# Second halves of the moving rows begin 1152 bytes on, with the padding behind each half

## The chip, the cores and the metric

One NeuronCore of one Trainium2 chip runs the whole program. The metric is the device time of one execution in microseconds (us); less is better. TensorE (PE in the rows) multiplies, VectorE (DVE) and ScalarE (ACT) do the elementwise work, GpSimd (POOL) does a little of it, and SyncE's queue (SP) issues the DMA transfers.

## The reference, cut to what matters

The reference is one inference step of a two-layer decoder trunk in float32, for 512 prompt tokens and 8 sample tokens that share all weights. Per layer:

```python
h = rmsnorm(x, W['norm_mix_w'][l])
(q, k, v, g, u, vm, om, ig, fg, z, xbc, dt, gate_r, gate_m, gate_s) = split_cols(h @ W['w_in'][l])
...
merged = (sigmoid(gate_r) * (y_r @ W['w_br_ret'][l])
          + sigmoid(gate_m) * (y_m @ W['w_br_ml'][l])
          + sigmoid(gate_s) * (y_s @ W['w_br_ssm'][l]))
x = x + merged @ W['w_out_mix'][l]
h = rmsnorm(x, W['norm_mem_w'][l])
x = x + mem_attention(h, mem_k, mem_v, W['mem_wq'][l], W['mem_wo'][l])
h = rmsnorm(x, W['norm_mlp_w'][l])
x = x + square(relu(h @ W['mlp_w1'][l])) @ W['mlp_w2'][l]
```

`y_r`, `y_m` and `y_s` come from three recurrent branches (retention, mLSTM, SSD). Nearly all arithmetic lies in the products of a 520-token activation with 1024-wide weight matrices.

## The kernel before, in words

Activations lie transposed: features on the 128 partitions, tokens along the free axis. The T = 520 columns are the L = 512 prompt tokens followed by the NB = 8 sample tokens. Products are made more exact than one float32r pass by splitting each operand into a high part and the remainder: `x = hi + lo`, `w = whi + wlo`, and the kernel sums `whi*xhi + whi*xlo + wlo*xhi`. The two parts of an activation stand in one tile, a "pair": `pair(tag)` (line 229) takes `[128, 2, 2, 576]` float32r, that is part (hi, lo), one of two row blocks, and a row of 576 columns of which the first 520 are used. Four tiles of the tag "h" and four of the tag "y" hold all such operands: the normed input, the branches' outputs, the merged gates, the attention's output, the hidden layer of the MLP. In the built program each of these tiles begins at a multiple of 256 bytes within a partition, and a row takes 2304 bytes.

`mmacc` (line 291) is the loop that nearly all PE work goes through. Per row block k it does three products (hi with hi, hi weights with lo input, lo weights with hi input), and each of them as two matmuls of HF = 260 columns, since a PSUM bank holds 512 float32:

```python
for j in range(2) if half is None else (half,):
    mm(ps[:, j, :HF] if half is None else ps[:, :HF], lhsT=w, rhs=x[:, j * HF:(j + 1) * HF],
```

So the matmuls alternate between a first half, read from the row's start, and a second half, read from byte 1040 of the row. Their results go to two PSUM banks. Every matmul loads its weights anew, also where the second half uses the same ones. `proj` (line 305) does 8 row blocks, 48 matmuls, into one such pair of banks. The MLP's second product (line 1788 on) does 4 row blocks, 24 matmuls. By these loops 19,872 matmuls of 260 columns read a pair's halves in alternation.

Three kinds of matmul read their moving operand otherwise. The mLSTM's q and k products from the tile `ucp` (in `proj_M`, lines 1016 to 1031) do six matmuls on one half and then six on the other, into one bank each; their rows are 520 columns with nothing between them. The memory keys (`mem_kv`, line 432 on) take 256 columns from row blocks of 256 columns, into one bank. The last group of the last layer's MLP (`last_group`, line 1727) takes columns 256 to 520 and then 0 to 256 of the pair's rows, into one bank.

The pairs are written by `split` (line 314: an ACT copy to hi, a DVE subtraction to lo), by `to_pair` (line 691), by `prep` and the merging of the gates (lines 1422 to 1435), and in the attention by lines 1515 and 1516. In most of them one ACT and one DVE instruction cover all 520 columns. In the retention and mLSTM branches and in the attention they cover the 512 prompt columns, and separate small DVE instructions write the 8 sample columns later.

PE's instructions stand in the order in which the program was written: a clock inside the recording (`clk`, advanced by each `mm`) decides when the generators of the branches put their instructions between the projections. The other engines' order is set by a scheduler from due times.

Of the kernel before, what the change touches and what calls it, by code (L numbers as in the profile page):

```python
# [17 lines left out]
NB = 8  # L18
T = L + NB
HF = T // 2  # L20
NT = 8
PITCH = 576
DEPTH = 2
C = 128
NC = L // C
# [87 lines left out]
def tile_trunk(ctx: ExitStack, tc: tile.TileContext, I, O):  # L113
# [69 lines left out]
    def tl(pool, shape, tag, bufs=None, dt=F32):  # L183
        return pool.tile(shape, dt, tag=tag, name=nm(tag), bufs=bufs)
# [42 lines left out]
    pmask = spar[:, 128:136]  # L227

    def pair(tag):
        return tl(act, [128, 2, 2, PITCH], tag, 4, F32R)[:, :, :, 0:T]  # L230

    def pieces(pairs):
        r = []
        for t in pairs:
            for k in range(2):
                r.append((t[:, 0, k, :], t[:, 1, k, :]))
        return r


    class Weights:  # L240
# [50 lines left out]
    def mmacc(ps, wl, xl, k0=0, k1=None, half=None, cols_=None):  # L291
        n = len(wl)
        for k in range(k0, n if k1 is None else k1):
            wh, wlo = wl[k]
            xh, xlo = xl[k]
            for m, (w, x) in enumerate(((wh, xh), (wh, xlo), (wlo, xh))):
                if cols_ is not None:
                    mm(ps, lhsT=w, rhs=x[:, cols_], start=(k == 0 and m == 0), stop=(k == n - 1 and m == 2))
                    continue
                for j in range(2) if half is None else (half,):  # L300
                    mm(ps[:, j, :HF] if half is None else ps[:, :HF], lhsT=w, rhs=x[:, j * HF:(j + 1) * HF],
                       start=(k == 0 and m == 0), stop=(k == n - 1 and m == 2))
            tick()

# [28 lines left out]
    def col(name, i):  # L333
        o = COLO[name] + i
        return cols[:, o:o + 1]
# [137 lines left out]
    def layer(l, mp, load_x):  # L473
# [17 lines left out]
        def g_norm():  # L491
            xt, ssq = yield from load_x()
            yield 4.0 if l else 2.2
            d = diag_cols(rms_cols([ssq.acc], 0, EPS))
            yield 5.29 if l else 4.3
            rb = rstd_row(d)
            for k in range(NT):
                hf = tl(un, [128, T], "yb", 2)
                V.scalar_tensor_tensor(out=hf, in0=xt[k], scalar=col("mix", k), in1=rb, op0=ALU.mult, op1=ALU.mult)
                split(hf, hx[k][0], hx[k][1])  # L500
                if l > 0:
                    st_.dma_start(out=xscr[:, k, :], in_=xt[k])

# [184 lines left out]
        def sel_b(b):  # L688
            return sel[:, b:b + 1].to_broadcast([128, 128])

        def to_pair(pt, k, f32t, s=None):
            s = slice(0, L) if s is None else s
            split(f32t, pt[:, 0, k, s], pt[:, 1, k, s])


        cs = tl(un, [128, 2080], "ucp", 1)
# [114 lines left out]
        def normalise(h, ysb, mv, rs, gt, kind, yps):  # L811
            nb = tl(sm, [128, NC], "nb", 2)
            V.scalar_tensor_tensor(out=nb, in0=mv[:, :, 0], scalar=-1.0, in1=rs, op0=ALU.mult, op1=ALU.mult)
            for c in range(NC):
                A.activation(out=ysb[:, c, 0:256], in_=ysb[:, c, 0:256], func=AF.Identity, scale=rs[:, c:c + 1], bias=nb[:, c:c + 1])
            yield 13.87
            stash = kind == "M" and not flags["br0"]
            if stash:
                while held[0] == 2:
                    yield 0.5  # L820
                held[0] += 1
                keep = tl(un, [128, 2, T], "gs", 2)
            else:
                yp = pair("y")
                yps[h] = yp
            for i in range(2):
                ps = pa([128, NC, 128])
                for c in range(NC):
                    tr(out=ps[:, c, :], in_=ysb[:, c, i * 128:(i + 1) * 128], identity=ident)
                yb = keep[:, i, :] if stash else tl(un, [128, T], "yb", 2)  # L830
                psf = ps.rearrange("p a b -> p (a b)")
                if kind == "R":
                    V.scalar_tensor_tensor(out=yb[:, 0:L], in0=psf, scalar=nwr[:, 2 * h + i:2 * h + i + 1], in1=gt[:, i, 0:L],
                                           op0=ALU.mult, op1=ALU.mult)
                else:
                    A.activation(out=yb[:, 0:L], in_=psf, func=AF.Copy, scale=nwr[:, 8 + 2 * h + i:9 + 2 * h + i])
                    V.scalar_tensor_tensor(out=yb[:, 0:L], in0=gt[:, i, 0:L], scalar=1.0, in1=yb[:, 0:L], op0=ALU.add, op1=ALU.mult)
                if not stash:
                    to_pair(yp, i, yb[:, 0:L])
            if stash:  # L840
                yield from unstash(keep, "br0", h, yps, slice(0, L))

        def unstash(keep, flag, h, yps, sl):
            while not flags[flag]:
                yield 0.5
            yps[h] = pair("y")
            for i in range(2):
                to_pair(yps[h], i, keep[:, i, sl], sl)
            held[0] -= 1

        def g_smp_R(h, vs, qkw):
# [52 lines left out]
        def smp_finish(ys, gs, nwo, yps):  # L904
            for i in range(2):
                V.tensor_tensor(out=ys[:, i, :, :], in0=ys[:, i, :, :],
                                in1=nwr[:, nwo:nwo + 8].rearrange("p (h i) -> p h i", i=2)[:, :, i:i + 1].to_broadcast([128, 4, NB]), op=ALU.mult)
            V.tensor_tensor(out=ys, in0=ys, in1=gs, op=ALU.mult)
            for h in range(4):
                V.tensor_copy(out=yps[h][:, 0, :, L:T], in_=ys[:, :, h, :])  # L910
                V.tensor_tensor(out=yps[h][:, 1, :, L:T], in0=ys[:, :, h, :], in1=yps[h][:, 0, :, L:T].bitcast(F32), op=ALU.subtract)

        def g_end_R(ints, smps, yps):
            while not all(s.done for s in smps):
# [78 lines left out]
        def proj_M(h):  # L993
# [22 lines left out]
            hi, lo = W.get(l, ("wqk", h))  # L1016
            q = tl(un, [128, 2, EXT], "pA", 1)
            k = tl(un, [128, 2, T], "pD", 1)
            xl = [(ucp[:, 0, i, :], ucp[:, 1, i, :]) for i in range(2)]
            for w in range(2):  # L1020
                for i in range(2):
                    sl = [slice(512 * w + 256 * kk + 128 * i, 512 * w + 256 * kk + 128 * i + 128) for kk in range(2)]
# [187 lines left out]
        def g_int_S(g, X, BC, sz, xs, s_smp, yps):  # L1210
# [115 lines left out]
            for i in range(2):  # L1326
                j = 2 * g + i
                yb = keep[:, i, :] if stash else tl(un, [128, T], "yb", 2)
                V.scalar_tensor_tensor(out=yb[:, 0:L], in0=yz[:, i, 0:L], scalar=col("ssmn", j), in1=p1, op0=ALU.mult, op1=ALU.mult)
                V.scalar_tensor_tensor(out=yb[:, L:T], in0=yz[:, i, L:T], scalar=col("ssmn", j), in1=p2, op0=ALU.mult, op1=ALU.mult)  # L1330
                if not stash:
                    to_pair(yp, i, yb, slice(0, T))
            if stash:
                yield from unstash(keep, "br1", g, yps, slice(0, T))

        def g_smp_S(g, xs, bcs):
            smp_scr(2, g, bcs, 2, 0.5)
# [72 lines left out]
        for j in range(8):  # L1410
            ph[0] = "br2."
            m0_ = tl(un, [128, T], "row", 2)
            ld.dma_start(out=m0_, in_=mscr[:, j, :])
            if j < 2:
                ps, wl = part[j]
                mmacc(ps, wl, yx, 6, 8)
                ps = ps[:, :, :HF]
            else:
                ps = proj(l, ("br", 2, j), yx)
            th = ths[j]  # L1420
            with soon():
                V.scalar_tensor_tensor(out=h2(th), in0=h2(th), scalar=1.0, in1=ps, op0=ALU.add, op1=ALU.mult)
            V.tensor_tensor(out=th, in0=th, in1=m0_, op=ALU.add)
            A.activation(out=mx[j][0], in_=th, func=AF.Copy, scale=0.5)
            V.scalar_tensor_tensor(out=mx[j][1], in0=th, scalar=0.5, in1=mx[j][0].bitcast(F32), op0=ALU.mult, op1=ALU.subtract)


        xs_ = XTiles()
# [2 lines left out]
        ax = pieces(ap_)  # L1431

        def prep(j, x, wname, dst, acc):
            A.activation(out=dst[j][0], in_=x, func=AF.Copy, scale=col(wname, j))
            V.scalar_tensor_tensor(out=dst[j][1], in0=x, scalar=col(wname, j), in1=dst[j][0].bitcast(F32), op0=ALU.mult, op1=ALU.subtract)
            acc.add(x)


# [25 lines left out]
        def g_att_p():  # L1464
# [44 lines left out]
            def outp(h, i):  # L1509
# [2 lines left out]
                for mt in range(2):  # L1512
                    mm(ps, lhsT=Vt[:, mt, i * 128:(i + 1) * 128], rhs=pT[h][:, mt, 0:512], start=(mt == 0), stop=(mt == 1))
                with soon():
                    A.activation(out=op[:, 0, i, 0:L], in_=ps, func=AF.Copy)
                    V.tensor_tensor(out=op[:, 1, i, 0:L], in0=ps, in1=op[:, 0, i, 0:L].bitcast(F32), op=ALU.subtract)  # L1516

            while 1 not in qs_ or not s_rq.done:
                yield 0.5
# [28 lines left out]
        def g_att_s(par):  # L1548
# [21 lines left out]
            for hi_, h in enumerate(heads):  # L1570
# [43 lines left out]
                        acc = tl(sm, [128, 2, NB], "o8", 2)  # L1614
                        yield 2.84
                with soon():
                    V.tensor_copy(out=op[:, 0, :, L:T], in_=acc)
                    V.tensor_tensor(out=op[:, 1, :, L:T], in0=acc, in1=op[:, 0, :, L:T].bitcast(F32), op=ALU.subtract)
                done_s.add(h)

        KT = []
# [142 lines left out]
        for g in range(9):  # L1764
            if g < 8:
                hps = [pair("h") for _ in range(2)]
                hid[g] = pieces(hps)
                pend = []
                for i in range(4):
                    ps = proj(l, ("w1", 4 * g + i), fx)  # L1770
# [5 lines left out]
                    for ps in pend:  # L1776
# [2 lines left out]
                        with soon():  # L1779
                            V.scalar_tensor_tensor(out=h2(rt), in0=ps, scalar=0.0, in1=h2(rbox[0]), op0=ALU.max, op1=ALU.mult)  # L1780
                        A.activation(out=rt, in_=rt, func=AF.Square)
                        split(rt, hid[g][ii][0], hid[g][ii][1])
                    pend = []
            if g > 0:
                hxg = hid.pop(g - 1)
# [214 lines left out]
```

## Time and profile before

| | |
|---|---|
| median of 3 runs | 2958.45 us (2951.89 to 2959.17) |
| the profiled execution | 2957.6 us |
| its span, first to last instruction | 2955.9 us |
| PE busy | 2900.0 us, 98% of the span |
| PE weight loads busy | 2826.5 us, 96% |
| DVE busy | 1865.5 us, 63% |
| ACT busy | 1309.0 us, 44% |
| granted TensorE clock, mean | 0.995 of full speed |

Busy times of PE are those of matmuls whose recorded durations overlap (a matmul of 260 columns is recorded as some 280 ns and the next one starts some 118 ns later), so PE's pace is read from the starts, not from the durations.

### The profile page before, as it was taken

To read this page: it belongs to the slowest core of one execution; us is meant where nothing else is said; L and a number is where in the kernel's file an instruction comes from. 1 tells how busy PE (TensorE), PEld (TensorE's weight loads), DVE (VectorE), ACT (ScalarE), POOL (GpSimd) and SP (SyncE) were. 2 spreads that over 40 slices of the span, in tenths; PEclk is the share of its full clock that TensorE was granted. 3 is DMA by queue.
4 is the path that set the end of the run, shared out by engine and by line. 5 is a ranking of instruction groups with operands and counts; after the bars stand their busy time and mean duration, and the time that the engine had idled before them with its cause. 6 is when DMAs were issued, how large, how long until landed. Compare 5 with 4: busy or idle time off the path is not lost. (4 is left out here: it accounts for less than half of the span.)

```text
span 2955.9 us, 57336 instructions
## 1 busy us (share of the span) xinstructions
PE 2900.0 (98%) x23334; PEld 2826.5 (96%) x23334; DVE 1865.5 (63%) x4254; ACT 1309.0 (44%) x2367; POOL 127.6 (4%) x388
## 2 busy tenths in 40 slices
PE   8999999999999999999999999999999999999998
PEld 7999999999999879999999999999999997899998
DVE  6677646776755665444576775568777556644445
ACT  5445445555533653322353454355545246432322
POOL 0001001100000000000000000010000000000000
PEclk9999999999999999999999999999999999999999
DMA  5445635454554642222454465445545445422221
GB/s 195 153 166 171 209 120 182 167 172 148 178 174 148 199 146 94 93 97 97 140 170 161 131 209 187 167 140 188 167 147 185 132 150 189 135 94 95 99 94 65
DMA packets 153112, 439.97 MB, mean 149 GB/s; under 512 B 18376, under 2 KB 31816, under 8 KB 152816
## 3 DMA queue, kind: packets, MB, share of 16 engines
q1 hardware_dynamic: 152848, 436.31, 44.8%
q8 instruction: 183, 3.00, 0.4%
q14 instruction: 81, 0.66, 0.1%
HBM read 380.43 MB, written 57.90 MB: 148 GB/s over the span
## 5 line engine op out<-in xcount | busy, mean ns | idle before, releaser
L272 ACT ACTIVATE mlp.wh<-mlp.raw 128x1024 fp32r<-128x1024 f32 x125 | 132.4, 1059 | 467.5 <-PE mlp.pp L170 451.6
L170 PE MATMUL mlp.pp<-mlp.h,mlp.wh 128*128 128x260 f32 (+2 forms) x1984 | 313.7, 280 | 0.0
L170 PE MATMUL mlp.pp<-kv.y,mlp.wh 128*128 128x260 f32 x1984 | 312.9, 280 | 0.0
L170 PEld LDWEIGHTS mlp.pp<-mlp.h,mlp.wh 128*128 128x128 f32 x1984 | 268.0, 188 | 0.0
L170 PEld LDWEIGHTS mlp.pp<-kv.y,mlp.wh 128*128 128x128 f32 x1984 | 266.9, 188 | 1.0 <-issue 1.0
L170 PE MATMUL mlp.pp<-mlp.h,mlp.wl 128*128 128x260 f32 (+2 forms) x992 | 199.0, 280 | 0.0
L170 PE MATMUL mlp.pp<-kv.y,mlp.wl 128*128 128x260 f32 x992 | 196.4, 280 | 0.0
L273 DVE TENSOR_TENSOR mlp.wl<-mlp.raw,mlp.wh 128x1024 fp32r<-128x1024 f32 x125 | 153.1, 1225 | 19.8 <-ACT mlp.wh L272 19.8
L1780 DVE SCALAR_TENSOR_TENSOR mlp.cc<-mlp.pp,rb.Cst 128x520 f32<-128x520 f32 x64 | 44.7, 699 | 180.1 <-PE mlp.pp L170 175.8
L170 PEld LDWEIGHTS mlp.pp<-mlp.h,mlp.wl 128*128 128x128 f32 x992 | 152.1, 188 | 0.0
L170 PEld LDWEIGHTS mlp.pp<-kv.y,mlp.wl 128*128 128x128 f32 x992 | 150.9, 188 | 0.0
L170 PE MATMUL Rp.pp<-mlp.h,Rp.wh 128*128 128x260 f32 x736 | 120.9, 286 | 2.2 <-DVE Rp.ext L719 2.0
L170 PE MATMUL Rp.pp<-h,Rp.wh 128*128 128x260 f32 x736 | 120.7, 286 | 1.5 <-DVE Rp.ext L719 0.8
L273 DVE TENSOR_TENSOR Mp.wl<-Mp.raw,Mp.wh 128x1024 fp32r<-128x1024 f32 x56 | 68.5, 1223 | 75.7 <-ACT Mp.wh L272 75.5
L170 PE MATMUL Sp.pp<-mlp.h,Sp.wh 128*128 128x260 f32 x640 | 105.0, 286 | 0.0
L170 PE MATMUL Sp.pp<-h,Sp.wh 128*128 128x260 f32 x640 | 104.9, 286 | 0.0
L272 ACT ACTIVATE br.wh<-br.raw 128x1024 fp32r<-128x1024 f32 x64 | 67.6, 1056 | 84.1 <-PE br.pp L170 81.9
L170 PEld LDWEIGHTS Rp.pp<-mlp.h,Rp.wh 128*128 128x128 f32 x736 | 101.4, 188 | 3.2 <-issue 2.2
L170 PE MATMUL Mp.pp<-mlp.h,Mp.wh 128*128 128x260 f32 x640 | 103.7, 284 | 0.0
L170 PEld LDWEIGHTS Rp.pp<-h,Rp.wh 128*128 128x128 f32 x736 | 101.0, 188 | 2.7 <-issue 1.0
L170 PE MATMUL Mp.pp<-h,Mp.wh 128*128 128x260 f32 x640 | 103.6, 284 | 0.0
L273 DVE TENSOR_TENSOR br.wl<-br.raw,br.wh 128x1024 fp32r<-128x1024 f32 x64 | 78.2, 1222 | 24.1 <-ACT br.wh L272 23.9
(826 smaller groups left out, 7882.3 us busy)
## 6 DMA issues: line engine op xcount, KB each, us to landing
mlp.raw<-wall SPq DMA_DIRECT2D x125, 512.0 KB, 3.5
br.raw<-wall SPq DMA_DIRECT2D x64, 512.0 KB, 3.6
Mp.raw<-wall SPq DMA_DIRECT2D x56, 512.0 KB, 3.5
Rp.raw<-wall SPq DMA_DIRECT2D x48, 512.0 KB, 3.6
Sp.raw<-wall SPq DMA_DIRECT2D x48, 512.0 KB, 3.6
Ms.st<-s_ml SPq DMA_DIRECT2D x32, 512.0 KB, 4.8
Ms.bc<-sscr SPq DMA_DIRECT2D x64, 256.0 KB, 4.7
o_mlC_s<-Ms.st SPq DMA_DIRECT2D x32, 512.0 KB, 4.9
```

The costliest lines, as they stand in the source:

```text
L170: PE.matmul(out, lhsT=lhsT, rhs=rhs, start=start, stop=stop)
L272: A.activation(out=hi[:, s], in_=t[:, s], func=AF.Copy)
L273: V.tensor_tensor(out=lo[:, s], in0=t[:, s], in1=hi[:, s].bitcast(F32), op=ALU.subtract)
L1780: V.scalar_tensor_tensor(out=h2(rt), in0=ps, scalar=0.0, in1=h2(rbox[0]), op0=ALU.max, op1=ALU.mult)
```

## The change

The row of 576 columns becomes two halves of HP = 288 columns, each with 260 used and 28 of padding. The second half now begins 1152 bytes after the first, in place of 1040. The tile's size, its place and the row pitch of 2304 bytes stay. All that reads or writes a pair follows:

- `mmacc` takes the half by an index of its own (`x[:, j, :]`), and `pieces` hands out views of shape `[128, 2, 260]`.
- Writers of all 520 columns write two runs of 260 in one instruction.
- Writers of the 512 prompt columns (retention, mLSTM, attention) write 260 and then 252 columns, in two instructions on ACT and two on DVE.
- The last group of the last layer's MLP keeps rows of 520 columns without a gap (`halved=False`).
- The tile `ucp` keeps its layout; it is only viewed as two halves.

```diff
@@ -18,8 +18,8 @@
 HF = T // 2
+HP = 288
 NT = 8
-PITCH = 576
@@ -227,14 +227,20 @@
     def pair(tag):
-        return tl(act, [128, 2, 2, PITCH], tag, 4, F32R)[:, :, :, 0:T]
-
-    def pieces(pairs):
+
+        return tl(act, [128, 2, 2, 2 * HP], tag, 4, F32R)
+
+    def halves(row):
+        return row.rearrange("p (j n) -> p j n", j=2)[:, :, 0:HF]
+
+    def pieces(pairs, halved=True):
         r = []
         for t in pairs:
             for k in range(2):
-                r.append((t[:, 0, k, :], t[:, 1, k, :]))
+                r.append(tuple(halves(t[:, s, k, :]) if halved else t[:, s, k, 0:T] for s in range(2)))
         return r
+
+    SMP = slice(L + HP - HF, T + HP - HF)
@@ -298,7 +304,7 @@
-                    mm(ps[:, j, :HF] if half is None else ps[:, :HF], lhsT=w, rhs=x[:, j * HF:(j + 1) * HF],
+                    mm(ps[:, j, :HF] if half is None else ps[:, :HF], lhsT=w, rhs=x[:, j, :],
@@ -688,9 +694,13 @@
-        def to_pair(pt, k, f32t, s=None):
-            s = slice(0, L) if s is None else s
-            split(f32t, pt[:, 0, k, s], pt[:, 1, k, s])
+        def to_pair(pt, k, f32t, samples=False):
+
+            if samples:
+                split(h2(f32t), halves(pt[:, 0, k, :]), halves(pt[:, 1, k, :]))
+                return
+            for a, b, o in ((0, HF, 0), (HF, L, HP - HF)):
+                split(f32t[:, a:b], pt[:, 0, k, a + o:b + o], pt[:, 1, k, a + o:b + o])
@@ -1512,8 +1522,7 @@
                 with soon():
-                    A.activation(out=op[:, 0, i, 0:L], in_=ps, func=AF.Copy)
-                    V.tensor_tensor(out=op[:, 1, i, 0:L], in0=ps, in1=op[:, 0, i, 0:L].bitcast(F32), op=ALU.subtract)
+                    to_pair(op, i, ps)
@@ -1764,7 +1773,7 @@
-                hid[g] = pieces(hps)
+                hid[g] = pieces(hps, halved=not (g == 7 and l == DEPTH - 1))
```

The other hunks replace `split(hf, ...)` by `split(h2(hf), ...)` and the slice `L:T` by `SMP` in the same way. PE's instructions are the same in number, shape and order; only their addresses differ. POOL's are the same as well. ACT and DVE get 48 instructions more each, from 48 splits of prompt columns.

One of the places where an instruction becomes two is the attention's output of the first head, on ACT. `Qp.h` is the pair, `Ap.pa` the PSUM tile that the attention's product was written to. Before:

```order
674 L1612 ACTIVATE br2.bcE_11247<-As.row_12396,As.mxs_12395 8x256
675 L1515 ACTIVATE Qp.h_11934<-Ap.pa_12403 128x512
676 L1493 ACTIVATE Ap.E_12415,Ap.sm_1846_12414<-Ap.pa_12408,Ap.mx_1845_12413,br2.rq_1647_11238 128x256 x2
677 L1599 ACTIVATE As.gs_11279,As.o_1842_12402<-As.gs_11279 128x256
678 L1496 ACTIVATE Ap.E_12415<-Ap.E_12415,Ap.sm_1846_12414 128x256 x2
679 L1515 ACTIVATE Qp.h_11934<-Ap.pa_12439 128x512
```

And after the change:

```order
693 L1621 ACTIVATE br2.bcE_11279<-As.row_12428,As.mxs_12427 8x256
694 L321 ACTIVATE Qp.h_11966<-Ap.pa_12435 128x260
695 L321 ACTIVATE Qp.h_11966<-Ap.pa_12435 128x252
696 L1503 ACTIVATE Ap.E_12449,Ap.sm_1846_12448<-Ap.pa_12442,Ap.mx_1845_12447,br2.rq_1647_11270 128x256 x2
697 L1608 ACTIVATE As.gs_11311,As.o_1842_12434<-As.gs_11311 128x256
698 L1506 ACTIVATE Ap.E_12449<-Ap.E_12449,Ap.sm_1846_12448 128x256 x2
699 L321 ACTIVATE Qp.h_11966<-Ap.pa_12473 128x260
700 L1608 ACTIVATE As.gs_11311,As.o_1842_12434<-As.gs_11311 128x256 x2
701 L321 ACTIVATE Qp.h_11966<-Ap.pa_12473 128x252
```

Each copy of 512 columns became two, and two of the sample stream's instructions now stand between the pieces of the second one.

## Rows read from the trace of the kernel before

**Rows 1.** The page's head: busy time, and the granted clock in 40 slices.

```profile
span 2955.9 us, 57336 instructions
...
PE 2900.0 (98%) x23334; PEld 2826.5 (96%) x23334; DVE 1865.5 (63%) x4254; ACT 1309.0 (44%) x2367; POOL 127.6 (4%) x388
...
PEclk9999999999999999999999999999999999999999
```

**Rows 2.** Timeline of PE in layer 1's MLP: start us, us, instructions merged, count.

```profile
2700.06 0.40 PE L170 MATMUL mlp.pp<-kv.y,mlp.wl 128*128 128x260 f32 x2
2700.29 0.63 PE L170 MATMUL mlp.pp<-kv.y,mlp.wh 128*128 128x260 f32 x4
2700.76 0.40 PE L170 MATMUL mlp.pp<-kv.y,mlp.wl 128*128 128x260 f32 x2
2700.99 0.63 PE L170 MATMUL mlp.pp<-kv.y,mlp.wh 128*128 128x260 f32 x4
2701.46 0.40 PE L170 MATMUL mlp.pp<-kv.y,mlp.wl 128*128 128x260 f32 x2
```

**Rows 3.** The same view in the third branch's output product of layer 1.

```profile
2349.73 0.40 PE L170 MATMUL br2.pp<-Si.y,br2.wl 128*128 128x260 f32 x2
2349.97 0.64 PE L170 MATMUL br2.pp<-Si.y,br2.wh 128*128 128x260 f32 x4
2350.45 0.40 PE L170 MATMUL br2.pp<-Si.y,br2.wl 128*128 128x260 f32 x2
...
2351.89 0.40 PE L170 MATMUL br2.pp<-Si.y,br2.wl 128*128 128x260 f32 x2
```

**Rows 4.** Busy time by stretches: from:to, us, PE, PEld, DVE, ACT, POOL busy (instructions), clock.

```profile
1140.00:1480.00 340.00, 340.00 (x2916) 340.00 (x2915) 166.76 (x194) 105.97 (x132) 0.00 (x0) 1.00 0.32 105
2340.00:2400.00 60.00, 60.00 (x502) 60.00 (x501) 33.03 (x42) 20.70 (x27) 0.00 (x0) 1.00 0.48 139
```

**Rows 5.** Timeline of PE: 256 columns, all read from multiples of 1024 bytes.

```profile
1484.14 0.28 PE L170 MATMUL kv.pp<-mlp.y,kv.wl 128*128 128x256 f32 x1
...
1485.22 0.28 PE L170 MATMUL kv.pp<-mlp.y,kv.wl 128*128 128x256 f32 x1
```

**Rows 6.** Timeline of PE in the last group: 264 columns from byte 1024 of a row.

```profile
2921.19 0.29 PE L170 MATMUL mlp.pp<-mlp.h,mlp.pC 128*128 128x264 f32 x1
...
2926.29 0.28 PE L170 MATMUL mlp.pp<-mlp.h,mlp.pC 128*128 128x264 f32 x1
```

**Rows 7.** Timeline of PE: q and k products from `ucp`, one half at a time.

```profile
265.06 0.28 PE L170 MATMUL Mp.pa<-Mp.ucp,Mp.wl 128*128 128x260 f32 x1
...
266.50 0.28 PE L170 MATMUL Mp.pa<-Mp.ucp,Mp.wl 128*128 128x260 f32 x1
```

**Rows 8.** Timeline of PE at the end: matmuls of one column, each with a weight load.

```profile
2929.79 0.58 PE L170 MATMUL fin.pa<-onesc,mlp.yb 128*128 128x1 f32 x4
2930.24 0.36 PE L170 MATMUL fin.pa<-onesc,mlp.cst 128*128 128x1 f32 x2
2930.46 0.58 PE L170 MATMUL fin.pa<-onesc,mlp.yb 128*128 128x1 f32 x4
```

**Rows 9.** Splits on ACT and DVE (lines 315, 316): duration ns min/median/max, first and last start.

```profile
L315 ACT ACTIVATE Ri.y<-Ri.yb x16: 612/632/635, 144.9 to 1726.3; 128x512 fp32r<-128x512 f32 x16
L315 ACT ACTIVATE mv.cc<-mv.row x4: 400/408/420, 947.6 to 2406.0; 128x256 fp32r<-128x256 f32 x4
L316 DVE TENSOR_TENSOR mlp.h<-mlp.cc,mlp.h x64: 690/700/702, 1132.1 to 2895.1; 128x520 fp32r<-128x520 f32 x64
L316 DVE TENSOR_TENSOR Ri.y<-Ri.yb,Ri.y x16: 672/683/684, 145.9 to 1727.0; 128x512 fp32r<-128x512 f32 x16
L316 DVE TENSOR_TENSOR mv.cc<-mv.row,mv.cc x4: 417/424/426, 948.0 to 2406.5; 128x256 fp32r<-128x256 f32 x4
```

**Rows 10.** Groups by line: an instruction of two runs of 260, read from two banks.

```profile
L1780 DVE SCALAR_TENSOR_TENSOR mlp.cc<-mlp.pp,rb.Cst 128x520 f32<-128x520 f32 x64 | 44.7, 699 | 180.1 <-PE mlp.pp L170 175.8
```

**Rows 11.** Who waited for the tile `Qp.h`, us and times.

```profile
  PEld wo.pp L170: 2.0, 5
  PE wo.pp L170: 0.4, 2
```

More of the change, by code (lines that the diff above doesn't have):

```diff
@@ L499, in g_norm @@
                 V.scalar_tensor_tensor(out=hf, in0=xt[k], scalar=col("mix", k), in1=rb, op0=ALU.mult, op1=ALU.mult)
-                split(hf, hx[k][0], hx[k][1])
+                split(h2(hf), hx[k][0], hx[k][1])
                 if l > 0:
@@ L840, in normalise, with unstash @@
             if stash:
-                yield from unstash(keep, "br0", h, yps, slice(0, L))
-        def unstash(keep, flag, h, yps, sl):
+                yield from unstash(keep, "br0", h, yps, False)
+        def unstash(keep, flag, h, yps, samples):
             while not flags[flag]:
@@ L847, in unstash @@
             for i in range(2):
-                to_pair(yps[h], i, keep[:, i, sl], sl)
+                to_pair(yps[h], i, keep[:, i, 0:T if samples else L], samples)
             held[0] -= 1
@@ L909, in smp_finish @@
             for h in range(4):
-                V.tensor_copy(out=yps[h][:, 0, :, L:T], in_=ys[:, :, h, :])
-                V.tensor_tensor(out=yps[h][:, 1, :, L:T], in0=ys[:, :, h, :], in1=yps[h][:, 0, :, L:T].bitcast(F32), op=ALU.subtract)
+                V.tensor_copy(out=yps[h][:, 0, :, SMP], in_=ys[:, :, h, :])
+                V.tensor_tensor(out=yps[h][:, 1, :, SMP], in0=ys[:, :, h, :], in1=yps[h][:, 0, :, SMP].bitcast(F32), op=ALU.subtract)
         def g_end_R(ints, smps, yps):
@@ L1018, in proj_M @@
             k = tl(un, [128, 2, T], "pD", 1)
-            xl = [(ucp[:, 0, i, :], ucp[:, 1, i, :]) for i in range(2)]
+            xl = [(h2(ucp[:, 0, i, :]), h2(ucp[:, 1, i, :])) for i in range(2)]
             for w in range(2):
@@ L1331, in g_int_S @@
                 if not stash:
-                    to_pair(yp, i, yb, slice(0, T))
+                    to_pair(yp, i, yb, True)
             if stash:
-                yield from unstash(keep, "br1", g, yps, slice(0, T))
+                yield from unstash(keep, "br1", g, yps, True)
         def g_smp_S(g, xs, bcs):
@@ L1423, in layer @@
             V.tensor_tensor(out=th, in0=th, in1=m0_, op=ALU.add)
-            A.activation(out=mx[j][0], in_=th, func=AF.Copy, scale=0.5)
-            V.scalar_tensor_tensor(out=mx[j][1], in0=th, scalar=0.5, in1=mx[j][0].bitcast(F32), op0=ALU.mult, op1=ALU.subtract)
+            A.activation(out=mx[j][0], in_=h2(th), func=AF.Copy, scale=0.5)
+            V.scalar_tensor_tensor(out=mx[j][1], in0=h2(th), scalar=0.5, in1=mx[j][0].bitcast(F32), op0=ALU.mult, op1=ALU.subtract)
         xs_ = XTiles()
@@ L1433, in prep @@
         def prep(j, x, wname, dst, acc):
-            A.activation(out=dst[j][0], in_=x, func=AF.Copy, scale=col(wname, j))
-            V.scalar_tensor_tensor(out=dst[j][1], in0=x, scalar=col(wname, j), in1=dst[j][0].bitcast(F32), op0=ALU.mult, op1=ALU.subtract)
+            A.activation(out=dst[j][0], in_=h2(x), func=AF.Copy, scale=col(wname, j))
+            V.scalar_tensor_tensor(out=dst[j][1], in0=h2(x), scalar=col(wname, j), in1=dst[j][0].bitcast(F32), op0=ALU.mult, op1=ALU.subtract)
             acc.add(x)
@@ L1616, in g_att_s @@
                 with soon():
-                    V.tensor_copy(out=op[:, 0, :, L:T], in_=acc)
-                    V.tensor_tensor(out=op[:, 1, :, L:T], in0=acc, in1=op[:, 0, :, L:T].bitcast(F32), op=ALU.subtract)
+                    V.tensor_copy(out=op[:, 0, :, SMP], in_=acc)
+                    V.tensor_tensor(out=op[:, 1, :, SMP], in0=acc, in1=op[:, 0, :, SMP].bitcast(F32), op=ALU.subtract)
                 done_s.add(h)
@@ L1781, in layer @@
                         A.activation(out=rt, in_=rt, func=AF.Square)
-                        split(rt, hid[g][ii][0], hid[g][ii][1])
+                        split(h2(rt) if len(hid[g][ii][0].shape) == 3 else rt, hid[g][ii][0], hid[g][ii][1])
                     pend = []
```

## The prediction

> **What bounds the kernel now.** I read the page's head first. PE is busy for 98% of the span at a granted clock of 0.9 or more in every slice [rows 1], so the full one of the clock's two levels, 2.4 GHz. DVE and ACT are far from full. What can make this kernel shorter or longer is thus PE's pace, and the next view is the timeline of PE, read by starts.
>
> There the pace takes two values. In layer 1's MLP six matmuls of 260 columns follow each other in 0.70 us: the rows with the low weights start at 2700.06, 2700.76 and 2701.46 [rows 2], which is 116.7 ns for one. In the third branch of the same layer the same six take 0.72 us, at 2349.73, 2350.45 and on to 2351.89 [rows 3], which is 120.0 ns. The view by stretches says the same over longer times: 2,916 matmuls in 340 us of the first MLP (116.6 ns), and 502 in 60 us of the second stretch (119.5 ns, or 120.0 once the two that overlap the edges are taken off) [rows 4]. Both have the same instruction, shape, tiles and clock. Nobody waits in either; the rhythm is PE's own.
>
> Counted by calls of 48 matmuls over the whole timeline (346 calls of that kind could be read, like those quoted), 127 lie within 0.3 ns of 116.7, 130 within 0.3 of 120.0, and 89 change from one to the other within the call, mostly where a transpose or a short matmul of a branch is put between. Their mean is 118.1 ns. A call keeps its rhythm until something interrupts it. The 19,872 matmuls that alternate between halves take 19,872 x 118.1 ns = 2,347 us of the 2,956 us span.
>
> What sets a pace of 116.7 to 120 when 260 columns at 2.4 GHz need 108.3? Two bounds lie just below. One is the columns. The other is the weight load, which every matmul has: where only one column is multiplied, four matmuls still take 0.45 us [rows 8], so 111.6 ns for one with hardly any columns to stream. The two run side by side, each near 110 ns, and together give 117 to 120, so they get in each other's way for 5 to 8 ns. The sum for the change hangs on whether the address of the second halves has a part in these 5 to 8 ns.
>
> **The change part by part.**
>
> *Second halves at 1152 in place of 1040.* 9,936 matmuls read from another address; PE's instructions are otherwise the same, in the same order. Row starts are multiples of 256 bytes, so first halves are aligned to 128 bytes now and second halves are not (1040 is 16 past a multiple of 128); afterwards both are. No row shows PE reading two aligned halves by turns, so I bound the price.
>
> From below: the quickest that rows allow is the weight load's 111.6 ns [rows 8]. (118.1 - 111.6) x 19,872 = 129 us less.
>
> From above: streams in which every start is a multiple of 128 bytes. 256 columns take 1.08 us for nine, 120.0 ns each [rows 5]; 264 columns from byte 1024 take 5.10 us for 42, 121.4 ns [rows 6]. At 121.4 ns the kernel loses (121.4 - 118.1) x 19,872 = 66 us.
>
> I take the value in between that the alternating halves themselves show at their best, 116.7 ns [rows 2]. These rows are nearest: same instruction, two banks by turns. The reason for taking the better rhythm is that two phases are possible only if successive reads start at different places within an aligned piece, which the 16 bytes bring; with equal starts each pair repeats the last. That picks one rhythm; that it picks the quick one is a choice, not a finding. Gain: (118.1 - 116.7) x 19,872 = **28 us**.
>
> Here a rule is weighed. The rows show that columns and weight loads disturb each other: 116.7 to 120.0 ns against 111.6 and 108.3 for each alone [rows 2, 3, 8]. The Trainium skill, page "TensorE: Matmul & The Clock Gate", section "Step-by-step: what each phase is for", says the opposite: PE has two independent read ports into SBUF, so loading the next weights takes no read bandwidth from the running matmul. By that rule no address could matter, and the term would be nothing. The trace disagrees with it by the 5 to 8 ns.
>
> *Prompt columns in two pieces.* 48 splits become 96 on each of two engines. On ACT one of 512 columns takes 632 ns and one of 256 takes 408 [rows 9], so two pieces take some 816: 184 ns more, 9 us over 48. On DVE 683 against two of 424 [rows 9]: 165 ns more, 8 us. PE covers nearly all of it: DVE and ACT have 1,000 us and more to spare [rows 1], and the pairs are written well ahead. The cover is thinnest at the attention's output, the last pair before the product `wo`: PE and its weight loads waited for it 2.4 us in total, seven times [rows 11]. Seven waits grown by the 0.35 us of one ACT and one DVE piece are 2.4 us, but the first piece now lets the DVE start earlier, so I take **1 us**. Bounds: nothing, and 17 us if PE waited for all of them.
>
> *Two runs of 260 in one instruction.* A DVE instruction that reads two runs from two banks takes 699 ns [rows 10], one over 520 plain columns 700 [rows 9]. So nothing. `last_group`, `ucp` and the DMAs keep their addresses and cost nothing.
>
> **Sum:** 2957.6 - 28 + 1 = 2930.6, say 2931 us, against the profiled execution's own 2957.6. The median of the runs is 0.9 us above that.
>
> **The rivals.**
>
> *The address has no part; the weight load and the clock beat set the pace.* For it: 256, 260 and 264 columns all run at 120 or 121.4 ns when half of one kind follows half of the same kind [rows 5, 7, 6], though their columns differ by 3 ns; and in `ucp`, where halves begin at 0, 16, 32 and 48 bytes past multiples of 64, the pace is 120.0 just as in the aligned stream. Against it: only streams that alternate between the two kinds of start reach 116.7. Then the two rhythms stay, newly dealt at each interruption. The MLP stages, now quick in both layers, could each fall to 120.0: some 3,000 matmuls x 3.3 ns = 10 us. So 2948 to 2970, likeliest 2958. The Trainium skill, page "SBUF — State Buffer", section "Door 1: The DMA port swizzle", bears on this: SBUF is read in lines of 16 bytes, and what costs is each step to a new line. Both 1040 and 1152 are multiples of 16, so by it nothing changes; no run so far tests it.
>
> *Slower: equal starts lock all pairs into the slow rhythm.* The one mechanism is that two aligned reads meet the weight reads, which are aligned too, at the same point each time. For it: every stream in the trace that is all aligned shows 120.0 or more and never 116.7 [rows 5, 6]. Against it: those streams write one bank, the pairs two, and `ucp` is not aligned and no quicker [rows 7]. It decides from the point where the mean pace passes 118.1. At 120.0: (120.0 - 118.1) x 19,872 = 38 us, so 2997 us; at 121.4, 3024.
>
> *A larger gain.* If the unaligned start were all that pushes the pace above the weight load, pairs would come down to 112 or 113 ns: 100 to 121 us less, so 2838 to 2858. Against it: the aligned streams again.
>
> **How the numbers follow.** A measurement here can tell about 0.3%, 9 us, from no change. Chances: my forecast 0.38 (its own range 2921 to 2944); a larger gain 0.08; the address without a part 0.29, of which a fresh deal gives 0.25 within the 9 us and 0.04 beyond it on the slow side; the slow lock 0.25. So faster 0.46, same 0.25, slower 0.29. Case by case the evidence is thin, hence a wide range: 2866 to 2999 takes in the forecast, the middle of the larger gains' way down, no change, and the lock at 120.0. Outside remain the larger gain (0.08) and a lock at 121.4 or so (0.06).
>
> **What would show each step.** Right: in the timeline of PE six paired matmuls take 0.70 us in all stages, also in the third branch and the projections. Wrong: six in 0.72 us in the MLP as well (the lock), or both rhythms in about equal parts (no part). The pieces are right if ACT's 260-column copies take about 410 ns, DVE's about 425, and PE's wait for `Qp.h` stays under 5 us. The prediction as a whole is wrong if PE's paired matmuls keep a mean of 118 ns or more.

## The result and the profile after

The changed kernel takes 2994.84 us in the median of four runs (2990.93 to 2996.6), the kernel before 2958.81 us beside it: a ratio of 1.012 with a 95% interval of 1.0104 to 1.0137, so 36 us slower. The forecast was 2931 us, faster. The rival that puts all pairs into the slow rhythm gave 2997 us.

The page's head after:

```profile
span 2991.5 us, 57439 instructions
...
PE 2935.9 (98%) x23334; PEld 2862.3 (96%) x23334; DVE 1870.3 (63%) x4302; ACT 1312.8 (44%) x2415; POOL 126.0 (4%) x388
...
PEclk9999999999999999999999999999999999999999
```

Against [rows 1] the span grew by 35.6 us and PE's busy time by 35.9, with the same 23,334 matmuls, the same 98% and the same granted clock in every slice. So PE does not wait more; its matmuls take longer. DVE and ACT have 48 instructions more each, as the split of the prompt columns says.

The timeline of PE in layer 1's MLP, the stage of [rows 2] (start us, us, instructions merged, count):

```profile
2735.10 0.40 PE L170 MATMUL mlp.pp<-kv.y,mlp.wl 128*128 128x260 f32 x2
2735.34 0.64 PE L170 MATMUL mlp.pp<-kv.y,mlp.wh 128*128 128x260 f32 x4
2735.82 0.40 PE L170 MATMUL mlp.pp<-kv.y,mlp.wl 128*128 128x260 f32 x2
2736.06 0.64 PE L170 MATMUL mlp.pp<-kv.y,mlp.wh 128*128 128x260 f32 x4
2736.54 0.40 PE L170 MATMUL mlp.pp<-kv.y,mlp.wl 128*128 128x260 f32 x2
```

The rows with the low weights now start 0.72 us apart (2735.10, 2735.82, 2736.54), where [rows 2] have 0.70. Busy time by stretches says it over 340 us of layer 0's MLP:

```profile
1140.00:1480.00 340.00, 340.00 (x2836) 340.00 (x2835) 158.71 (x184) 102.90 (x128) 0.00 (x0) 1.00 0.30 98
```

That is 2,836 matmuls where [rows 4] have 2,916: 119.9 ns for one in place of 116.6. Over the whole trace, the 19,872 paired matmuls take 2,449 us from start to start, before 2,411. That is 38 us more, the whole loss; the rest of the program takes some 3 us less. Leaving out the 2% of intervals of 130 ns and more, where something else came between, their mean is 119.99 ns after and 118.10 before. Nearly every call now keeps to 120.0: all 590 stretches of 24 paired matmuls (half a call of `proj`, or one of the MLP's second product) that nothing interrupts lie within 0.3 ns of it, where before 206 of 590 did and 383 lay as close to 116.7. The quick rhythm is gone.

The other two terms, in the views of the splits' lines (duration ns min/median/max, first and last start) and of the groups:

```profile
L321 ACT ACTIVATE Ri.y<-Ri.yb x32: 397/406/423, 141.1 to 1748.0; 128x260 fp32r<-128x260 f32 x16, 128x252 fp32r<-128x252 f32 x16
...
L322 DVE TENSOR_TENSOR Ri.y<-Ri.yb,Ri.y x32: 409/419/426, 142.1 to 1748.9; 128x260 fp32r<-128x260 f32 x16, 128x252 fp32r<-128x252 f32 x16
```

```profile
L1789 DVE SCALAR_TENSOR_TENSOR mlp.cc<-mlp.pp,rb.Cst 128x520 f32<-128x520 f32 x64 | 44.8, 700 | 189.8 <-PE mlp.pp L170 185.3
```

The pieces take 406 and 419 ns, against the 408 and 424 that the prediction read from copies of 256 columns [rows 9]. The read over two banks keeps its 700 ns [rows 10]. But two pieces cost less than twice one where they follow each other directly, since the recorded time of the second begins before that of the first ends. From the timeline, the first two on ACT and on DVE (start us, us):

```profile
141.13 0.71 ACT L321 ACTIVATE Ri.y<-Ri.yb 128x260 fp32r<-128x260 f32 x2
142.10 0.76 DVE L322 TENSOR_TENSOR Ri.y<-Ri.yb,Ri.y 128x260 fp32r<-128x260 f32 x2
```

From the start of the first to the end of the second it is 0.71 and 0.76 us, where the prediction added up 0.82 and 0.85. Who waited for the tile `Qp.h` (us, times):

```profile
  PEld wo.pp L170: 2.2, 6
  PE Ap.pa L170: 2.0, 2
  PE wo.pp L170: 1.0, 2
  PE As.pa L177: 0.4, 2
```

PE and its weight loads waited 5.6 us in total, against 2.4 in [rows 11]. The rows with `Ap.pa` and `As.pa` are new: these are matmuls into the attention's own PSUM tiles. The two pieces are read from such tiles (`Ap.pa`), so by the names these matmuls wait for a tile until a piece has been read from it.

### The profile page after: what moved, and what is told of

Its sections match the earlier page's. It is cut to its first block, busy times and chain, and to the rows that moved or that the text cites. A ratio compares the mean times of both kernels' runs of the same rounds, so it can differ in the third digit from the quotient of the medians.

```text
span 2991.5 us, 57439 instructions
## 1 busy us (share of the span) xinstructions
PE 2935.9 (98%) x23334; PEld 2862.3 (96%) x23334; DVE 1870.3 (63%) x4302; ACT 1312.8 (44%) x2415; POOL 126.0 (4%) x388
## 5 line engine op out<-in xcount | busy, mean ns | idle before, releaser
L170 PE MATMUL mlp.pp<-mlp.h,mlp.wh 128*128 128x260 f32 (+2 forms) x1984 | 319.7, 283 | 0.0
L170 PE MATMUL mlp.pp<-kv.y,mlp.wh 128*128 128x260 f32 x1984 | 318.9, 283 | 0.0
```

Source lines behind the costliest of these rows:

```text
L170: PE.matmul(out, lhsT=lhsT, rhs=rhs, start=start, stop=stop)
```

## The experiments

All kernels are the changed one with two numbers: H0, the element at which the first halves begin in their row, and HO, that of the second halves (one element is 4 bytes). The weights and the rows of the pairs begin at multiples of 256 bytes, so "place" below means the bytes by which a half begins past such a multiple, counted modulo 128. Before has the places (0, 16) and the change (0, 0). The pace is the mean of the paired matmuls' intervals under 130 ns, of one trace. Most kernels were run once, beside one run of the kernel before (2956.7 to 2957.8 us). The kernels at 1072 and 1088 write the same edit with HO alone.

The common edit, with the numbers of the first run:

```diff
 HP = 288
+H0, HO = 0, 260
@@ def halves(row):
-        return row.rearrange("p (j n) -> p j n", j=2)[:, :, 0:HF]
+        d = HO - H0
+        return row[:, H0:H0 + 2 * d].rearrange("p (j n) -> p j n", j=2)[:, :, 0:HF]
@@ def pieces(pairs, halved=True):
-... t[:, s, k, 0:T] for s in range(2)))
+... t[:, s, k, H0:H0 + T] for s in range(2)))
@@
-    SMP = slice(L + HP - HF, T + HP - HF)
+    SMP = slice(L + HO - HF, T + HO - HF)
@@ def to_pair(pt, k, f32t, samples=False):
-            for a, b, o in ((0, HF, 0), (HF, L, HP - HF)):
+            for a, b, o in ((0, HF, H0), (HF, L, HO - HF)):
```

**The address undone, the pieces kept** (`H0, HO = 0, 260`: second halves at byte 1040 again).

> Second halves back at byte 1040, all else as changed (prompt columns in two pieces, instructions of two runs). If the address alone made the loss: both rhythms return, mean pace near 118 ns, time 2955 to 2965 us. If the pieces have a part in it: above 2965 us, with a mean pace of 118 ns and longer waits of PE for Qp.h and the y tiles.

Measured: 2961.54 us, before 2957.3; pace 118.08 ns, both rhythms as before. In layer 0's MLP there are again the 2,916 matmuls of [rows 4]:

```profile
1140.00:1480.00 340.00, 340.00 (x2916) 340.00 (x2915) 166.01 (x193) 106.06 (x132) 0.00 (x0) 1.00 0.32 104
```

So the loss lies in the address, and the pieces cost a few microseconds at most.

**Second halves at byte 1056** (`H0, HO = 0, 264`), with padding, and 32 past a multiple of 128.

> Second halves at byte 1056 (32 past a multiple of 64), a gap of 16 bytes behind the first halves. Theory 'equal starts' (two halves that begin at the same place within 64 bytes lock at 120.0 ns): no lock, mean pace 116.7 to 118.5, 2930 to 2965 us. Theory 'gap' (only a second half that follows the first directly can go at 116.7): locked at 120.0, some 2995 us.

Measured: 2943.43 us and 117.07 ns: quicker than before. Padding as such thus costs nothing. In the stretch of the third branch, before has 502 matmuls in 60 us [rows 4]; at 1056 there are 517, the quick rhythm in this stage too, while the first stretch, quick before, stays as it was:

```profile
1140.00:1480.00 340.00, 340.00 (x2915) 340.00 (x2914) 168.68 (x206) 106.48 (x132) 0.00 (x0) 1.00 0.33 106
2340.00:2400.00 60.00, 60.00 (x517) 60.00 (x516) 34.62 (x52) 23.77 (x35) 0.00 (x0) 1.00 0.50 153
```

**Second halves at byte 1104** (`H0, HO = 0, 276`), 80 past a multiple of 128, 16 past one of 64.

> Second halves at byte 1104 (16 past a multiple of 64, as 1040 is), a gap of 64 bytes. 'Equal starts': as before the change, both rhythms, mean pace near 118, 2945 to 2965 us. 'Gap': locked at 120.0, some 2995 us.

Measured: 2995.94 us, 120.15 ns, 2,826 matmuls in the 340 us of layer 0's MLP:

```profile
1140.00:1480.00 340.00, 340.00 (x2826) 340.00 (x2825) 158.34 (x183) 102.62 (x127) 0.00 (x0) 1.00 0.30 97
```

The two halves do not start equal, neither modulo 128 nor 64, and the pace is as slow as in the change. So a slow pace does not need equal starts.

**Both halves off the aligned places** (`H0, HO = 4, 276`: bytes 16 and 1104, places 16 and 80).

> As the run with 1104, but first halves begin at byte 16 too, so both halves are 16 past a multiple of 64. 'Equal starts': locked at 120.0, some 2995 us. Theory 'aligned starts' (it is the multiple of 64 that locks): no lock, mean pace 118.5 or less, at most 2965 us. 'Gap': locked, some 2995 us.

Measured: 3006.97 us, 120.64 ns.

```profile
1140.00:1480.00 340.00, 340.00 (x2811) 339.52 (x2810) 158.26 (x187) 102.95 (x128) 0.00 (x0) 1.00 0.29 95
```

No half begins on a multiple of 128, and the kernel is slower still. So a slow pace does not need an aligned start either. Two theories were left: D, by which the distance between the halves modulo 128 sets the pace (16, 32, 80, 64 and 0 so far), and W, by which each half's own place against the weights does. The next four runs were made for these.

**Distance of the quick run, both halves shifted by 32** (`H0, HO = 8, 272`: places 32 and 64).

> First halves begin 32 bytes, second halves 64 bytes past a multiple of 128 (distance 1056 as in e2, both shifted by 32). Theory D (only the distance between the two halves, modulo 128, sets the pace): the pace of e2, mean 117.1 ns per paired matmul, about 2943 us. Theory W (each half's own place against the weights, which begin at multiples of 256, sets it): another pace, 118 to 120.7 ns, 2957 to 3007 us.

Measured: 2984.79 us, 119.80 ns.

```profile
1140.00:1480.00 340.00, 340.00 (x2835) 340.00 (x2835) 159.18 (x184) 102.33 (x126) 0.00 (x0) 1.00 0.30 99
```

The same distance, and 80 matmuls fewer than the 2,915 of the run at 1056. D falls here. W is left, and the later expectations part it in two: what counts is a half's place relative to the weights (R), or its absolute place (A).

**Second halves at 1072, 1088 and 1120** (`H0, HO = 0, 268`, `0, 272` and `0, 280`: places 48, 64 and 96).

> Second halves 48 bytes past a multiple of 128, first halves aligned. Both theories only know neighbours: 32 past gave 117.1 ns, 80 past 120.15. If the quick place is a range below 64, about 117 ns and 2943 us; if 32 alone is quick, 118 to 120 ns and 2957 to 2995 us.

> First halves aligned, second halves 64 bytes past a multiple of 128: the distance of e4, which had both 16 bytes further. Theory D: as e4, 120.6 ns and about 3007 us. Theory W: not as e4, away from 120.6 ns by half a nanosecond or more, so outside 2997 to 3017 us.

> Second halves 96 bytes past a multiple of 128, first halves aligned; the distance is 32 short of a multiple where e2's is 32 over it. Theory D with the sign of the distance of no account (two reads by turns, each the other's neighbour): as e2, 117.1 ns and 2943 us. Theory W, or D with a sign: between the neighbours at 80 (120.15 ns) and 128 (120.0 ns), about 2995 us.

Measured: 2992.21 us (119.93 ns), 2967.46 us (118.51 ns) and 2990.24 us (119.64 ns). Of the three, that at 1088:

```profile
1140.00:1480.00 340.00, 340.00 (x2876) 340.00 (x2875) 162.82 (x189) 104.23 (x129) 0.00 (x0) 1.00 0.31 102
```

Its distance is that of (16, 80), which was 39.5 us slower: D falls again. Nor is there a quick range: 16 and 48 bytes lie on both sides of 32, and both are slower.

**The weights' part: the halves held, the weights moved.** A small unused tile ahead of the others is made 32 bytes shorter, so that all tiles after it, the weights and the pairs too, begin 32 bytes lower. With `H0, HO = 8, 272` the halves then stand at the absolute places of the quick run, but 32 and 64 past the weights. With `H0, HO = 0, 264` they stand 0 and 32 past the weights, at other absolute places.

```diff
-    const.tile([128, 32], F32, name="gap")
+    const.tile([128, 24], F32, name="gap")
```

> Every tile, the weights among them, begins 32 bytes lower (32 before a multiple of 256); the pairs' halves are moved up by 32 within their tiles, so they stand where e2 has them (0 and 32 past a multiple of 128), and 32 and 64 past the weights, as in f2. Theory R (a half's place relative to the weights counts): as f2, mean pace 119.8 ns, about 2985 us. Theory A (its absolute place counts, wherever the weights stand): as e2, 117.1 ns, about 2943 us.

> All tiles 32 bytes lower, halves within their tiles as in e2: 0 and 32 past the weights, but 96 and 0 past a multiple of 128. Theory R: as e2, 117.1 ns, about 2943 us. Theory A: a pair not run yet (96, 0); its neighbours (0, 96) and (32, 64) gave 119.6 and 119.8 ns, so 2980 to 2992 us.

Measured: 2991.78 us and 119.92 ns for the first, 2942.95 us and 117.09 ns for the second. The first:

```profile
1140.00:1480.00 340.00, 340.00 (x2836) 340.00 (x2835) 158.53 (x184) 101.73 (x125) 0.00 (x0) 1.00 0.30 98
```

The second:

```profile
1140.00:1480.00 340.00, 340.00 (x2916) 340.00 (x2915) 166.62 (x198) 105.27 (x130) 0.00 (x0) 1.00 0.32 107
```

Both come out as theory R says. The first has its halves where the run at 1056 has them, and the same instructions; of what PE reads in them, only where the weights begin differs, and it loses some 80 matmuls in this stretch. Every tile behind the shortened one moved, not the weights alone, so the pace could hang on what the other engines read and write meanwhile. The trace of the first run speaks against that: in two stretches of this MLP, one with DVE and ACT idle and one with both busy nearly throughout, PE runs the same number of matmuls, and the DMA share differs too (0.51 and 0.09):

```profile
1427.30:1430.70 3.40, 3.40 (x31) 3.40 (x30) 0.00 (x0) 0.00 (x0) 0.00 (x0) 1.00 0.51 154
1442.30:1445.70 3.40, 3.40 (x31) 3.40 (x30) 3.05 (x4) 3.37 (x6) 0.00 (x0) 1.00 0.09 11
```

Over the 340 us, six paired matmuls in a row take 120.0 ns each where DVE, ACT and POOL all stand still and where at least one of them works throughout; in the run at 1056 they take 116.7 in both conditions. What is left is what PE itself reads: the pace hangs on where a half begins against the weights. The Trainium skill, page "TensorE: Matmul & The Clock Gate", section "Step-by-step: what each phase is for", has two independent read ports, for the moving operand and for the weights; these two runs disagree with an independence of the two, by 2.8 ns a matmul.

**A start inside a line of 16 bytes, and a shift by 16** (`H0, HO = 0, 262`: byte 1048, place 24; `4, 268`: places 16 and 48).

> Second halves 24 bytes past a multiple of 128, between 16 (118.1 ns, both rhythms) and 32 (117.1 ns), and not a multiple of 16. If the place counts in lines of 16 bytes, 24 begins within the line that begins at 16 and ends within one more: 118.1 ns or slower, 2955 to 2995 us. If it counts by bytes: between the two, 117.1 to 118.1 ns, 2943 to 2958 us.

> Halves 16 and 48 past a multiple of 128; distance 32 as in e2 and f2. If the quick rhythm needs the first halves level with the weights, it is gone: 119 to 120.7 ns, 2975 to 3007 us, as f2 with 119.8. If f2 was slow by its 64 alone, about 117 ns and 2943 us.

Measured: 3020.04 us and 121.66 ns for the first, 2970.71 us and 118.58 ns for the second. The first:

```profile
1140.00:1480.00 340.00, 340.00 (x2793) 339.52 (x2792) 157.43 (x193) 102.38 (x127) 0.00 (x0) 1.00 0.29 95
```

Eight bytes on from before's 1040 and eight short of the quick 1056 lies the slowest kernel so far, beyond the 2995 us that the expectation allowed. Bytes do not count smoothly. In all but three kernels the paces at which most calls sit are 116.67, 118.33, 120.0 and 121.67 ns: steps of 1.67 ns, which at 2.4 GHz is four columns, or 16 bytes of a row. The three lie between: places 0 and 80 (most at 120.2 to 120.8), 16 and 80 (most at 120.83), and 96 and 0 (121.1). By the Trainium skill, page "SBUF — State Buffer", section "Door 1: The DMA port swizzle", SBUF is read in lines of 16 bytes and each step to a new one costs. A row of 260 columns from byte 1048 touches 66 such lines in place of 65, and there the trace agrees. But between multiples of 16 the rule sees no difference, and with the first halves level these differ by up to 3.3 ns (117.1 at 1056, 120.4 at 1136, below). The second run has neither the quick pace nor the 119 to 120.7 ns expected without it: with the first halves 16 off the weights' place the quick rhythm is gone, though less is lost than at 32.

**The better offset and the pieces, timed several times; two more places.** The kernels of 1056 and of 1040 with pieces, as above, and `H0, HO = 24, 288` (places 96 and 0) and `0, 284` (places 0 and 112).

> The kernel of e2 (second halves at 1056), timed. Theory R: quick rhythm throughout, 1.0 ns x 19,872 = 20 us less than before, less the cost of the pieces and of longer interruptions (about 6 us): 2941 to 2945 us, ratio 0.994 to 0.996, faster than both kernels. A rival, that e2's one look was a lucky deal of rhythms: 2950 us or more in some of the runs.

> The kernel of e1 (offset 1040, prompt columns in two pieces), timed: the price of the pieces by itself. The prediction's term: 1 us, so 2959 to 2961 us, ratio 1.0003 or so. Rival: the 4 us of e1's one look is real, 2961 to 2963 us, ratio 1.0014.

> First halves 96 bytes past the weights' multiple of 256, second halves level with it; distance 1056, 32 modulo 128, as in e2, f2 and g3, which gave 117.1, 119.8 and 118.6 ns as the first halves stood 0, 32 and 16 past. If the quick rhythm needs the first halves level with the weights: slow, 119 to 120.7 ns, 2975 to 3007 us. If it is enough that one of the two is level and they are 32 apart: 117 ns, 2943 us.

> Second halves 112 bytes past a multiple of 128, first halves level with the weights; the last multiple of 16 that was not run. Neighbours: 96 gave 119.6 ns, 128 gave 120.0. By them 119 to 120.5 ns, 2975 to 3003 us. A second quick place here would be 117 ns, 2943 us.

Measured, beside a median of 2958.54 us for before:

- 1056: 2942.51 us in the median of six runs (2938.99 to 2950.48), ratio 0.9953, interval 0.9941 to 0.9965. It beats both kernels: 16 us under the kernel before, 52 under the change. One of six runs lay at 2950, as the rival of a lucky deal has it, but with the lowest granted clock of the six (0.992 of full speed, the others 0.993 to 0.996). Both traces that were taken at 1056 show the quick rhythm nearly throughout: 575 of 585 and 578 of 587 uninterrupted stretches of 24 matmuls lie within 0.3 ns of 116.7.
- 1040 with pieces: 2961.94 us, ratio 1.0016, interval 1.0006 to 1.0025. The pieces cost 3.4 us by the medians and 4.7 by the ratio, between 1.8 and 7.4 by its interval.
- Places 96 and 0: 3022.54 us, the slowest of all, beyond the 3007 us that the expectation allowed. That the halves are 32 apart with one of them level is thus not enough.
- Place 112: 2997.18 us, 120.41 ns. No second quick place there.

The page's head of the timed kernel at 1056:

```profile
span 2940.9 us, 57439 instructions
...
PE 2881.9 (98%) x23334; PEld 2807.1 (95%) x23334; DVE 1869.9 (64%) x4302; ACT 1312.1 (45%) x2415; POOL 124.7 (4%) x388
```

Its span is 15.0 us below that of [rows 1]; its 19,872 paired intervals sum to 2,394 us, 17 below before's. The gain is PE's pace, less what the pieces cost. The slowest of the table, places 96 and 0, has 2,805 matmuls where the quick ones have 2,916:

```profile
1140.00:1480.00 340.00, 340.00 (x2805) 339.52 (x2804) 159.41 (x195) 103.30 (x129) 0.00 (x0) 1.00 0.30 95
```

All places in one table:

| first, second half: place against the weights | pace, ns | time, us |
|---|---|---|
| 0, 32 (1056) | 117.1 | 2942.5 (median of six) |
| 0, 32, all tiles 32 lower | 117.1 | 2943.0 |
| 0, 16 (before: 1040) | 118.1, two rhythms | 2958.5 |
| 0, 64 (1088) | 118.5 | 2967.5 |
| 16, 48 | 118.6 | 2970.7 |
| 0, 96 (1120) | 119.6 | 2990.2 |
| 32, 64 | 119.8 | 2984.8 |
| 32, 64, all tiles 32 lower | 119.9 | 2991.8 |
| 0, 48 (1072) | 119.9 | 2992.2 |
| 0, 0 (the change: 1152) | 120.0 | 2994.8 |
| 0, 80 (1104) | 120.2 | 2995.9 |
| 0, 112 (1136) | 120.4 | 2997.2 |
| 16, 80 | 120.6 | 3007.0 |
| 0, 24 (1048) | 121.7 | 3020.0 |
| 96, 0 | 121.1, and 1,032 longer intervals | 3022.5 |

The kernel before is not the only one with two rhythms. At 32 and 64, 43 of 591 uninterrupted stretches of 24 matmuls run at 116.7 ns and the others at 120; at 16 and 48, 66 of 588 run at 120 and the others at 118.3.

## Why the prediction was wrong

- **PE's pace is what moves the time: right.** Every kernel of the table has the same matmuls at nearly the same clock (0.993 to 0.996 of full speed in the traces), and the time follows the pace of the paired matmuls, but for the few microseconds by which single runs differ. So was the reading that columns and weight loads get in each other's way: with the halves at 32 and 64 past the weights the pace is 119.8 ns where the halves were moved and 119.9 where the weights were.
- **Term 1, the address: the step that failed.** It took the value of [rows 2] for the aligned pair, 116.7 ns and 28 us less. Measured are 120.0 ns and 38 us more. That equal starts leave one rhythm came out, but it is nothing that marks equal starts: places (0, 32), (0, 48) and (0, 64) differ, and each keeps nearly to one rhythm too. What failed is the choice of the quick one. It went by instruction and banks ("nearest: same instruction, two banks by turns"), while the rows that shared the property which the change sets, aligned starts, were [rows 5] and [rows 6], both at 120 ns or more. By [rows 5] the term would have been the 38 us that came; those rows have 256 columns and one bank, so that they hit the number may be chance.
- **Term 2, the pieces: right in kind, too small.** It took 1 us out of bounds of 0 to 17; the runs at 1040 show 3.4 to 4.7 us. The sum there left out a case that its own rows suggested: it counted 2.4 us more if all waits for `Qp.h` grew, and took less because the first piece comes earlier. In the change, and in the same way in both traces at 1040 with pieces, these waits went from 2.4 to 5.6 us, 3.2 more, and part of them is a new kind, the matmuls into `Ap.pa` and `As.pa`. On ACT and DVE themselves the pieces cost less than was worked out: 3.8 and 4.8 us more of busy time, where 9 and 8 were put down, since pieces that follow directly overlap.
- **Term 3, two runs of 260: right,** 700 ns as before.
- **The rival that came true** gave 2997 us: 120.0 ns for all pairs. Its price and its partner, the weight reads, hold. Its condition does not: halves that are both level are slow, but so are the second halves at 48, 64, 80, 96 and 112, by 0.4 to 2.3 ns against before. Equal starts are one of many slow cases, so its mechanism, that both halves meet the weight reads at the same point, is not shown.
- **The rival with no part for the address** described the kernel before rightly. Its rhythm is newly dealt: the kernel at 1040 with pieces ran the third branch quick in one execution and slow in another. In the first there were 516 matmuls in the 60 us:

```profile
2340.00:2400.00 60.00, 60.00 (x516) 60.00 (x516) 33.38 (x42) 20.18 (x26) 0.00 (x0) 1.00 0.51 151
```

And in the second, the timed one, 502, as in [rows 4]:

```profile
2340.00:2400.00 60.00, 60.00 (x502) 60.00 (x501) 32.26 (x41) 21.09 (x27) 0.00 (x0) 1.00 0.46 139
```

But the change shows no dealing, so the address has a part.

- **The range** of 2866 to 2999 held the time, by 4 us; it reached as far as the lock at 120.0 ns because that had its own chance of 0.25.

What stays open is which reads meet: why 32 bytes past is quick with the first halves level, and why four columns' time is lost or won at a time. No run shows an operand's reads one by one. That places repeat every 128 bytes was assumed in counting them and not tried on its own.

## What to carry to other kernels

A stream of matmuls with a weight load each can change its pace by 4% with nothing but the address at which the moving operand begins against the weights: read the pace from starts, and if it takes several values at one clock and one shape, try offsets in steps of 16 bytes before anything else. Round, aligned places are no safe choice: the best offset here was 32 bytes past one, and no rule tried predicted it. A lesson of this one case: where a trace offers several nearest rows for an unknown price, take the ones that share the property that the change sets, not those that share the instruction.

## What the hardware showed that was not expected

- Two operands' relative place sets the pace. 32 bytes on the weights' side cost 2.8 ns a matmul, 117.1 to 119.9 ns, at the same moving addresses.
- In most kernels the pace sits on steps of 1.67 ns (116.67, 118.33, 120.0, 121.67 ns; three kernels lie between), and it does not follow the bytes smoothly: second halves at 1040, 1048 and 1056 give 118.1, 121.7 and 117.1 ns.
- Two halves with the same distance, 32 modulo 128, give 117.1, 118.6, 119.8 and 121.1 ns as the first stands 0, 16, 32 or 96 bytes past the weights' place.
